# The weights' ring as one tile with 16-byte steps between its buffers, and x moved by 8 bytes for the second layer's experts

## The chip, the cores and the metric

The kernel runs on one core of one Trainium2 chip. The metric is the device time of one execution in microseconds. The core's engines run their own instruction streams and wait for one another by semaphores: PE (TensorE) multiplies matrices, DVE (VectorE), ACT (ScalarE) and POOL (GpSimd) work element by element, and SP (SyncE) issues the DMAs. PE's work appears twice in a profile: PEld is the load of a matrix of weights into the array, PE the matmul that streams the other operand through it. On-chip memory (SBUF) has 128 partitions; an address here is a byte offset inside a partition, the same in all of them. PSUM takes the matmuls' results.

## The reference

Two layers work on 256 frames of width 1024. Layer 0 mixes with multi-head latent attention, layer 1 with sparse attention whose keys a small indexer picks. Each is followed by a PEER mixer, which is where most of the time goes, and each result is added to 1.41 times the input and normalised:

```python
for i in range(DEPTH):
    m = _mla_mixer(x, ...) if i % N_MIXERS == 0 else _dsa_mixer(x, ...)
    x = _layernorm(DN_ALPHA * x + m, ln_gain[i, 0], ln_bias[i, 0])
    f = _peer(x, peer_w_q[i], peer_sub_keys[i], peer_w_down[i], peer_w_up[i])
    x = _layernorm(DN_ALPHA * x + f, ln_gain[i, 1], ln_bias[i, 1])

def _peer(x, w_q, sub_keys, w_down, w_up):       # 16384 experts, 8 heads
    q = (xt @ w_q).reshape(T, PEER_HEADS, 2, PEER_QDIM // 2)
    ...                                          # top 16 of two key tables, top 16 of their sums
    u = w_down[e_blk]
    a = jnp.einsum('td,ted->te', x_blk, u)
    hg = jax.nn.gelu(a, approximate=False) * g_blk
    return jnp.einsum('te,ted->td', hg, w_up[e_blk])
```

## The kernel before

**Dense experts.** The kernel doesn't gather the chosen experts. It multiplies x by all 16384 rows of `w_down` (128 blocks of 128 experts), applies the GELU, multiplies by a matrix that holds each frame's gates at its chosen experts and zero elsewhere, and multiplies the result by all of `w_up`. So each layer has 128 blocks of "down" (results named `d`) and 128 of "up" (results named `y`), and between the blocks of `d` the small fp16 matmuls `G` that place the gates.

**Split operands.** Each matmul of float32 data is made of three in the faster format fp32r: an operand is split into a high part, a copy rounded to fp32r, and a low part, the difference. `mm3` (line 258) issues high by high, high by low and low by high. x's parts are `xh` and `xl` (lines 194 and 195, 8 chunks of 256 columns each). In the down stage (`proj`, line 264) the weights' 128 columns are loaded into the array and x's 256 columns of one chunk are streamed: per block 8 chunks times 3, 24 matmuls of 256 columns. In the up stage (`rows`, line 289) x's place is taken by two blocks at a time of the gated GELU, split by `operand` (line 1109) into slots of `xh` and `xl`; they are loaded as weights, and 512 columns of the ring's block are streamed: 2 groups of frames, 3 passes, 2 halves, 12 matmuls of 512 columns per block.

**The ring.** All weights run through one `Stream` (line 52), in the order in which `ws.add` names them. A block of 128 x 1024 is loaded by a DMA on SP's queue into one of four `raw` buffers (`_load`, line 70), copied by ACT into a `hi` tile and subtracted by DVE (some blocks by POOL) into a `lo` tile (`_split`, line 88; `open` and `close`, lines 110 and 124, do the same in an order written out by hand for the blocks around a normalisation). `hi` and `lo` come from two pools of four buffers (lines 170 and 171), each 4096 bytes long; a new tile waits for the last reader of the tile that had its buffer. `get` (line 104) hands out a block and splits those up to three ahead. The first block is split by hand in `first` (line 1142) from tiles made at lines 1132 to 1134, and is cut off the stream's list at line 1138. `share` (line 97) gives every third block to POOL during the query projection of layer 1.

**What sets the order.** Each engine executes its stream in order, and the tile framework adds the waits that the reads and writes ask for. Around a normalisation (`finish`, line 381) the order is written by hand: the last four blocks of the projection run for the first 128 frames, then for the second; the new x is transposed by PE (`Turned`, line 355), split into `xh` and `xl`, and multiplied into the next stage's first four blocks. `out_proj` (line 660) calls `finish` for both attentions, with `start` 0 for layer 0 and 4 for layer 1. In both attentions the heads' outputs are kept in `xh` and `xl` as well (`oh, ol = xh, xl`, lines 689 and 822), since x itself is no longer needed there.

**Other operands.** In layer 0's query projection the matmuls `qn` and `qr` stream the normalised latent from four small tiles `V` and `U` (pool `ohp`, line 721) with weights from the ring. Apart from these two and the two attentions' inner matmuls, all large matmuls pair a buffer of the ring with `xh` or `xl`.

Of the kernel before, what the change touches and what calls it, by code (L numbers as in the profile page):

```python
# [11 lines left out]
F32R = mybir.dt.float32r  # L12
# [6 lines left out]
P = 128  # L19
T = 256  # L20
D = 1024
NC = D // P
# [22 lines left out]
WARM = 9  # L45
EARLY = 11264
GSCALE = 2.0 ** 14
DSA_POOL = 3
MAGIC = 12582912.0


class Stream:
# [13 lines left out]

    def add(self, src, w=D):
        self.blocks += [(src[i], w) for i in range(src.shape[0])]

    def _load(self, upto):  # L70
        while self.n_loaded <= min(upto, len(self.blocks) - 1):
            src, w = self.blocks[self.n_loaded]
            if self.n_loaded in self.early:
                t = self.early[self.n_loaded]
            else:
                t = self.raw.tile([P, D], F32, tag="raw", name=f"raw{self.n_loaded}")
                self.last = self.nc.sync.dma_start(t[:, :w], src).ins
            self.tiles.append(t)
            self.n_loaded += 1
# [8 lines left out]
    def _split(self, upto, pooled=False):  # L88
        nc = self.nc
        while self.n_split <= min(upto, len(self.blocks) - 1):  # L90
            w = self.blocks[self.n_split][1]
            self._load(self.n_split)
            raw = self.tiles[self.n_split][:, :w]
            hi = self.hi.tile([P, D], F32R, tag="hi", name=f"hi{self.n_split}")[:, :w]
            lo = self.lo.tile([P, D], F32R, tag="lo", name=f"lo{self.n_split}")[:, :w]
            self.act(lambda: nc.scalar.copy(hi, raw))  # L96
            if pooled or self.share and self.n_split % self.share == 0:
                nc.gpsimd.tensor_tensor(lo, raw, hi.bitcast(F32), op=ALU.subtract)
            else:
                self.dve(lambda: nc.vector.tensor_tensor(lo, raw, hi.bitcast(F32), op=ALU.subtract))  # L100
            self.ready.append((hi, lo))
            self.n_split += 1
# [7 lines left out]
    def open(self, queue):  # L110

        i = self.n_split
        assert i == self.n_taken
        self._load(i)
        raw = self.tiles[i]
        hi = self.hi.tile([P, D], F32R, tag="hi", name=f"hi{i}")
        lo = self.lo.tile([P, D], F32R, tag="lo", name=f"lo{i}")
        queue("act", lambda: self.nc.scalar.copy(hi, raw))
        self.ready.append((hi, lo))
        self.n_split += 1  # L120
        self.n_taken += 1
        return i
# [39 lines left out]
def tile_trunk(ctx: ExitStack, tc: tile.TileContext, ins, out: bass.AP):  # L162
    nc = tc.nc
    def pool(name, bufs, **kw):
        return ctx.enter_context(tc.tile_pool(name=name, bufs=bufs, **kw))

    lead = pool("lead", 1)
    wide = pool("wide", 1)
    raws = pool("raws", 4)
    his = pool("his", 4)  # L170
    los = pool("los", 4)
    big = pool("big", 1)
    const = pool("const", 1)
    dram = pool("dram", 1, space=bass.MemoryType.DRAM)
# [16 lines left out]
    ones = lead.tile([P, 16], F32, tag="ones", name="ones")[:, 0:1]  # L191
    mhalf = lead.tile([P, 16], F32, tag="mhalf", name="mhalf")[:, 0:1]
    keep = [dram.tile([P, D], F32, tag=f"x{t}", name=f"x{t}") for t in range(2)]
    xh = wide.tile([P, NC, T], F32R, tag="xh", name="xh")
    xl = wide.tile([P, NC, T], F32R, tag="xl", name="xl")
    place16 = const.tile([P, 2, T], F16, tag="place16", name="place16")
    gate16 = const.tile([P, T], F16, tag="gate16", name="gate16")
    rest = const.tile([P, T], F32, tag="rest", name="rest")
# [11 lines left out]
    nc.vector.memset(ones, 1.0)  # L210
    nc.vector.memset(mhalf, -0.5)

    ws = Stream(nc, raws, his, los)
    ws.add(ins["mla_h"][0:6])
    ws.add(ins["mla_qk"])
    ws.add(ins["mla_v"])
# [72 lines left out]
    def rows(o4, lhs, blk, start, stop, tiles=(0, 1)):  # L289

        h, l = blk
        lh, ll = lhs
        for t in tiles:
            tsl = slice(t * P, (t + 1) * P)
            todo = [(w, rr, i, n) for i, (w, rr) in enumerate(((lh, h), (lh, l), (ll, h))) for n in range(2)]
            if stop:
                todo.sort(key=lambda z: z[3])
            for w, rr, i, n in todo:
                ins = mm(o4[t][n], w[:, tsl], rr[:, n * 512 : (n + 1) * 512], start and i == 0, stop and i == 2)
        return ins  # L300

    def queue_of():

        last = {}

        def queue(engine, emit):
            with ExitStack() as order:
                if engine in last:
                    order.enter_context(tc.issue_after(last[engine]))
                ins = emit()  # L310
            last[engine] = ins.ins
            return ins

        return queue
# [66 lines left out]
    def finish(y4, lhs_of, n, g, b, x, spare, lead=None):  # L381

        blks = [ws.get(ahead=0) for _ in range(STAGGER)]
        queue = queue_of()
        last = None
        norms = []
        for t in range(2):  # L390
            with ExitStack() as order:
                if last is not None:
                    order.enter_context(tc.issue_after(last.ins))
                for i, blk in enumerate(blks):
                    k = n - STAGGER + i
                    last = rows(y4, lhs_of(k), blk, k == 0, k == n - 1, (t,))
            norms.append(Norm(queue, x[t], y4[t], g, b, spare[t], spare[2 + t], spare[4]))
        n0, n1 = norms
        n0.sums()
        n0.square()  # L400
        n0.centre()
        n0.scale()
        n0.result()
        if lead is None:
            n1.sums()
            n1.square()
            n1.centre()
            n1.scale()
            n1.result()
            for t in range(2):  # L410
                for h, q in enumerate((nc.sync, nc.scalar)):
                    s = slice(h * 512, (h + 1) * 512)
                    q.dma_start(out[t * P : (t + 1) * P, s], spare[t][:, s])
            return
        nc.sync.dma_start(keep[0], spare[0])
        queue("pe", lambda: last)
        x0, x1 = Turned(queue, 0, spare[0]), Turned(queue, 1, spare[1])
        blk = [ws.open(queue) for _ in range(3)]
        n1.sums()
        x0.high(0, 2)  # L420
        x0.high(1, 4)
        n1.square()
        x0.low(0)
        n1.centre()
        blk.append(ws.open(queue))
        n1.scale()
        x0.low(1)
        n1.result()
        nc.sync.dma_start(keep[1], spare[1])
        unit = lead(queue)  # L430

        def do(t, part, *ks):
            for k in ks:
                unit(t, part, k, ws.ready[blk[k]])

        do(0, "hh", 0, 1, 2)
        do(0, "lh", 0, 1, 2)
        do(0, "hh", 3)
        do(0, "lh", 3)
        x1.high(0, 2)  # L440
        x1.high(1, 4)
        do(1, "hh", 0, 1, 2, 3)
        ws.close(blk[0], queue)
        ws.close(blk[1], queue)
        x1.low(0)
        do(0, "hl", 0, 1)
        do(1, "lh", 0, 1)
        do(1, "hl", 0, 1)
        ws.close(blk[2], queue)
        x1.low(1)  # L450
        do(0, "hl", 2)
        do(1, "hl", 2)
        do(1, "lh", 2)
        ws.close(blk[3], queue)
        do(0, "hl", 3)
        do(1, "hl", 3)
        do(1, "lh", 3)
# [202 lines left out]
    def out_proj(oh, ol, g, b, x, spare, start):  # L660
        for h in range(start, HEADS - STAGGER):
            for t in range(2):
                project(oh, ol, h, t)
        y4 = begun.pop("y4")
        finish(y4, lambda h: (oh[:, h, :], ol[:, h, :]), HEADS, g, b, x, spare, lead_queries)

    def load_mask(ar):
# [139 lines left out]
    def dsa():  # L807
# [82 lines left out]
        for t in range(2):  # L890
            for n in range(2):
                nc.scalar.copy(v[:, t, n * 512 : (n + 1) * 512], v4[t][n])
        ws.share = DSA_POOL
        for h in range(0, HEADS, 2):
# [22 lines left out]
    def peer(li):  # L917
# [77 lines left out]
        def choose():  # L995
# [40 lines left out]
            gt, i1 = tail[:, 0:T], tail[:, T : 2 * T]  # L1036
            nc.vector.tensor_scalar(gt, pg[:, :T], GSCALE, None, op0=ALU.mult)
            nc.vector.tensor_copy(gate16, gt)
# [23 lines left out]
        def place(g4, done):  # L1062
# [8 lines left out]
            if done < P:  # L1071
                nc.scalar.mul(A[:, done:, tsl], pv[:, done:, :], 1.0 / GSCALE)
            if done:
                nc.vector.scalar_tensor_tensor(A[:, :done, tsl], pv[:, :done, :], 1.0 / GSCALE, A[:, :done, tsl],
                                               op0=ALU.mult, op1=ALU.mult)
# [54 lines left out]
    xt = Arena(arena, 30720).take(NC, T)  # L1130
    piece = [slice(c, c + 2) for c in range(0, NC, 2)]
    raw0 = raws.tile([P, D], F32, tag="raw", name="raw0")
    hi0 = his.tile([P, D], F32R, tag="hi", name="hi0")
    lo0 = los.tile([P, D], F32R, tag="lo", name="lo0")
    nc.sync.dma_start(raw0, ins["mla_h"][0])
    for c in range(0, NC, 4):
        last = nc.sync.dma_start(xt[:, c : c + 4, :], ins["xT"][c // 4])
    ws.blocks = ws.blocks[1:]
    with tc.issue_after(last.ins):
        ws._load(2)  # L1140

    def first(o):

# [129 lines left out]
```

## Time and profile before

| what | value |
|---|---|
| median of 2 runs | 1838.18 us (1838.15 to 1838.22) |
| span of the profiled execution | 1836.6 us |
| layer 0's `d` stage, first to last matmul | 147.3 to 548.6 us |
| layer 0's `y` stage | 548.4 to 896.6 us |
| layer 1's `y` stage begins | 1480.8 us |
| HBM traffic over the span | 182 GB/s |

The profile is of one execution with a span of 1836.6 us, from the first to the last recorded instruction. Its groups of instructions name the line that issues them, the result and the operands by the program's tile names, the shape, the count, the busy time of the group and the mean duration of one. A matmul's recorded duration is longer than the distance from one to the next, because they are pipelined; what a stage costs is that distance times the count. Line 253 is the helper that records all matmuls, so groups have to be told apart by the tiles' names. In these groups the matmul of `d` lists `xh` first and the ring's buffer second, whichever is streamed.

### The profile page before, as it was taken

Reading aid. Unit: us, or ns where it says so; the run is one execution under the profiler, and the core shown is the slowest. Engines: PE = TensorE matmul, PEld = TensorE weight load, DVE = VectorE, ACT = ScalarE, POOL = GpSimd, SP = SyncE. Lnnn points to the kernel's source line nnn. Section 1 sums busy time; section 2 is a strip of 40 time slices with the busy share of each in tenths; the row PEclk is TensorE's granted clock in tenths of the full one; section 3 lists DMA queues with packets and bytes.
Section 4 is the critical chain, followed back from the end, with each engine's and each line's share of the span. In section 5 each row is a group of like instructions: output and inputs, shape, how many; then the busy total and the mean of one; then the engine's idle time right before and its main releaser. Section 6 shows DMA issues by size and latency. Waiting matters only on the chain.

```text
span 1836.6 us, 32394 instructions
## 1 busy us (share of the span) xinstructions
PE 1824.8 (99%) x12495; PEld 1671.9 (91%) x12495; DVE 1317.8 (72%) x2348; ACT 1056.2 (58%) x1834; POOL 362.8 (20%) x265
## 2 busy tenths in 40 slices
PE   9999999999999999999999999999999999999998
PEld 8899999999998888888889899999999988888886
DVE  6689986788865555555688789957888765555555
ACT  6655456887764444444466555548877654444443
POOL 2002442445510000000022004504455300000000
PEclk9999999999999999999999999999999999999999
DMA  7554555444456555555646445554444475555553
GB/s 240 195 179 167 184 184 172 162 161 152 161 174 237 192 192 194 193 194 195 210 157 227 164 165 182 173 193 161 154 157 155 168 235 192 194 193 194 195 195 116
DMA packets 93468, 335.47 MB, mean 183 GB/s; under 512 B 10368, under 2 KB 11392, under 8 KB 93312
## 3 DMA queue, kind: packets, MB, share of 16 engines
q1 hardware_dynamic: 93024, 332.87, 52.9%
q8 instruction: 98, 1.61, 0.4%
q14 instruction: 58, 0.48, 0.1%
q10 hardware_dynamic: 288, 0.52, 0.1%
HBM read 329.16 MB, written 4.19 MB: 182 GB/s over the span
## 4 chain that ended last, share of the span: by engine, by line
PE 98%; DVE 1%; issue 1%; ACT 0%; DMA 0%; SPq 0%; DVEq 0%; POOLq 0%; POOL 0%; ACTq 0%
PE d L253 40%; PE y L253 40%; PE pq L253 4%; PE G L253 3%; PE q L253 3%; PE v L253 1%; PE qw L253 1%; PE s L253 1%; PE ps L253 1%; PE h L253 1%; PE qi L253 1%; PE o L253 1%; PE qn L253 0%; DMA arena<-in_xT 0%; PE kn L253 0%
## 5 line engine op out<-in xcount | busy, mean ns | idle before, releaser
L100 DVE TENSOR_TENSOR lo<-raw,hi 128x1024 fp32r<-128x1024 f32 (+1 forms) x579 | 763.9, 1321 | 345.0 <-ACT hi L96 344.1
L96 ACT CAST hi<-raw 128x1024 fp32r<-128x1024 f32 (+1 forms) x583 | 611.0, 1049 | 561.7 <-PE d L253 265.3
L253 PE MATMUL d<-xh,hi 128*128 128x256 f32 x2048 | 585.1, 286 | 0.0
L253 PE MATMUL d<-xh,lo 128*128 128x256 f32 x2048 | 579.2, 283 | 0.0
L253 PE MATMUL d<-xl,hi 128*128 128x256 f32 x2048 | 579.2, 283 | 0.0
L253 PEld LDWEIGHTS d<-xl,hi 128*128 128x128 f32 x2048 | 392.7, 192 | 0.0
L253 PEld LDWEIGHTS d<-xh,lo 128*128 128x128 f32 x2048 | 392.6, 192 | 0.0
L253 PEld LDWEIGHTS d<-xh,hi 128*128 128x128 f32 x2048 | 392.5, 192 | 0.0
L253 PE MATMUL y<-lo,xh 128*128 128x512 f32 x1088 | 337.7, 389 | 0.0
L253 PE MATMUL y<-hi,xh 128*128 128x512 f32 x1088 | 337.7, 390 | 0.0
L253 PE MATMUL y<-hi,xl 128*128 128x512 f32 x1088 | 337.3, 389 | 0.0
L1055 POOL TENSOR_TENSOR gate<-hot,gate 128x512 f16<-128x512 f16 x128 | 221.8, 1751 | 310.6 <-DVE hot L1053 310.6
L253 PEld LDWEIGHTS y<-lo,xh 128*128 128x128 f32 x1088 | 204.2, 188 | 42.7 <-DVE lo L100 0.3
L253 PEld LDWEIGHTS y<-hi,xl 128*128 128x128 f32 x1088 | 204.2, 188 | 42.4
L253 PEld LDWEIGHTS y<-hi,xh 128*128 128x128 f32 x1088 | 203.8, 188 | 41.8
L347 POOL TENSOR_TENSOR st<-st,mhalf 128x1 f32<-128x1 f32 x8 | 4.4, 551 | 827.2 <-DVE st L345 827.2
L1059 ACT ACTIVATE gate<-hot,rest 128x128 f16<-128x128 f16 x512 | 166.1, 413 | 0.9 <-DVE hot L1053 0.9
L1114 ACT CAST xh<-arena 128x512 fp32r<-128x512 f32 x128 | 79.8, 623 | 145.6 <-PE y L253 145.4
L1115 DVE TENSOR_TENSOR xl<-arena,xh 128x512 fp32r<-128x512 f32 x128 | 88.2, 692 | 73.5 <-ACT xh L1114 73.5
L1053 DVE TENSOR_TENSOR hot<-iota,place 128x1024 f16<-128x1024 f16 x128 | 84.9, 703 | 49.1 <-PE G L253 49.0
L1024 POOL TENSOR_TENSOR arena<-arena 128x800 f32<-128x800 f16 x32 | 78.8, 2482 | 38.8 <-DVE arena L1022 38.0
L253 PE MATMUL G<-gate,hot 128*128 128x128 f16 x1024 | 70.1, 221 | 0.0
(222 smaller groups left out, 1739.5 us busy)
## 6 DMA issues: line engine op xcount, KB each, us to landing
raw<-in_down SPq DMA_DIRECT2D x256, 512.0 KB, 3.2
raw<-in_up SPq DMA_DIRECT2D x256, 512.0 KB, 4.3
raw<-in_peer_q SPq DMA_DIRECT2D x24, 512.0 KB, 4.4
raw<-in_dsa_qk SPq DMA_DIRECT2D x16, 512.0 KB, 3.2
raw<-in_mla_w_o SPq DMA_DIRECT2D x8, 512.0 KB, 5.9
arena<-in_peer_q SPq DMA_DIRECT2D x8, 512.0 KB, 4.3
raw<-in_dsa_v SPq DMA_DIRECT2D x8, 512.0 KB, 4.3
raw<-in_dsa_w_o SPq DMA_DIRECT2D x8, 512.0 KB, 3.7
```

Source lines behind the costliest of these rows:

```text
L96: self.act(lambda: nc.scalar.copy(hi, raw))
L100: self.dve(lambda: nc.vector.tensor_tensor(lo, raw, hi.bitcast(F32), op=ALU.subtract))
L253: return pe(lambda: nc.tensor.matmul(o, l, r, start=start, stop=stop, skip_group_check=True))
L347: nc.gpsimd.tensor_tensor(st[:, 5:6], st[:, 4:5], mhalf, op=ALU.pow)
L1024: nc.gpsimd.tensor_tensor(o.rearrange("p k c -> p c k"), same, cell[t][:, h, :, None].to_broadcast([P, CELLS, TOPK]), op=ALU.mult)
L1053: nc.vector.tensor_tensor(hot, iota4[:, None].to_broadcast([P, 2, P, 4]), place16[:, :, None, four].to_broadcast([P, 2, P, 4]), op=ALU.is_ ...
L1055: nc.gpsimd.tensor_tensor(gate[:, 0], hot[:, 1].rearrange("p c j -> p j c"), gate16[:, four, None].to_broadcast([P, 4, P]), op=ALU.mult)
L1059: nc.scalar.mul(gate[:, 1, j, :], hot[:, 1, :, j], rest[:, t : t + 1])
L1114: nc.scalar.copy(hh, a)
L1115: nc.vector.tensor_tensor(al, a, hh.bitcast(F32), op=ALU.subtract)
```

## The change

The two pools of four tiles become two tiles, `hi` and `lo`, each with room for four buffers of 1024 columns and 64 columns more. Block i of the stream lies in buffer i modulo 4, at 4096 bytes times its number and 16 bytes times its number further. `xh` and `xl` become two halves of one tile, and a second pair of views of the same tile begins 2 columns, 8 bytes, later; `out_proj` of layer 1 turns to these views before its `finish`, so that the new x, layer 1's query projection and its experts use them. The heads' outputs that this projection reads stay in the first views. The first block is counted as block 0 of the stream now, so the indices of the others grow by one, and the test for POOL's blocks takes one off.

```diff
+RING = 4
+SKEW = 4
...
+    def parts(self, i):
+        skew = i % RING * SKEW
+        at = i % RING * D + skew
+        return [ring[:, at : at + self.blocks[i][1]] for ring in (self.hi, self.lo)]
...
-            hi = self.hi.tile([P, D], F32R, tag="hi", name=f"hi{self.n_split}")[:, :w]
-            lo = self.lo.tile([P, D], F32R, tag="lo", name=f"lo{self.n_split}")[:, :w]
+            hi, lo = self.parts(self.n_split)
             self.act(lambda: nc.scalar.copy(hi, raw))
-            if pooled or self.share and self.n_split % self.share == 0:
+            if pooled or self.share and (self.n_split - 1) % self.share == 0:
...
-    his = pool("his", 4)
-    los = pool("los", 4)
+    rings = pool("rings", 1)
...
-    xh = wide.tile([P, NC, T], F32R, tag="xh", name="xh")
-    xl = wide.tile([P, NC, T], F32R, tag="xl", name="xl")
+    xs = wide.tile([P, 2 * NC * T + 64], F32R, tag="xs", name="xs")
+    views = [xs[:, at : at + 2 * NC * T].rearrange("p (b c t) -> p b c t", c=NC, t=T) for at in (0, 2)]
+    xh, xl = views[0][:, 0], views[0][:, 1]
...
-    ws = Stream(nc, raws, his, los)
+    ring = [rings.tile([P, RING * D + 64], F32R, tag=k, name=k) for k in ("hi", "lo")]
+    ws = Stream(nc, raws, *ring)
...
         y4 = begun.pop("y4")
+        nonlocal xh, xl
+        if start:
+            xh, xl = views[1][:, 0], views[1][:, 1]
         finish(y4, lambda h: (oh[:, h, :], ol[:, h, :]), HEADS, g, b, x, spare, lead_queries)
...
-    hi0 = his.tile([P, D], F32R, tag="hi", name="hi0")
-    lo0 = los.tile([P, D], F32R, tag="lo", name="lo0")
...
-    ws.blocks = ws.blocks[1:]
+    hi0, lo0 = ws.parts(0)
+    ws.n_loaded = ws.n_split = ws.n_taken = 1
+    ws.tiles.append(raw0)
+    ws.ready.append((hi0, lo0))
     with tc.issue_after(last.ins):
-        ws._load(2)
+        ws._load(3)
```

`open` takes its `hi` and `lo` from `parts` in the same way as `_split`.

More of the change, by code (lines that the diff above doesn't have):

```diff
@@ L115, in open @@
         raw = self.tiles[i]
-        hi = self.hi.tile([P, D], F32R, tag="hi", name=f"hi{i}")
-        lo = self.lo.tile([P, D], F32R, tag="lo", name=f"lo{i}")
+        hi, lo = self.parts(i)
         queue("act", lambda: self.nc.scalar.copy(hi, raw))
```

## The prediction

> **What bounds the kernel now.** I read the page's busy rows first, then its slices, then the chain of work that ended last.
>
> ```profile
> span 1836.6 us, 32394 instructions
> PE 1824.8 (99%) x12495; PEld 1671.9 (91%) x12495; DVE 1317.8 (72%) x2348; ACT 1056.2 (58%) x1834; POOL 362.8 (20%) x265
> PEclk9999999999999999999999999999999999999999
> PE 98%; DVE 1%; issue 1%; ACT 0%; DMA 0%; SPq 0%; DVEq 0%; POOLq 0%; POOL 0%; ACTq 0%
> ```
>
> PE is busy in 99% of the span at full granted clock, and 98% of the chain is PE. So the time is a number of matmuls times the distance from one start to the next, and waits of the other engines cost nothing today. A busy PE is not PE at its peak, so the next view is the chain in order of time (start, us, what, count), where a group's time over its count is that distance.
>
> ```profile
> 23.94 2.16 PE krope L253 x18
> 26.10 4.10 PE qn L253 x36
> 35.20 4.25 PE qr L253 x36
> 151.56 146.63 PE d L253 x1222
> 548.60 348.19 PE y L253 x1536
> 1083.91 146.63 PE d L253 x1222
> ```
>
> An experts' first matmul d (256 columns) starts every 146.63/1222 = 0.1200 us in both layers; a second one, y (512 columns), every 348.19/1536 = 0.2267 us. The 256 columns between them cost 106.7 ns, so a column costs 0.417 ns, and both shapes carry the same rest: 120.0 - 106.7 = 13.3 ns and 226.7 - 213.4 = 13.3 ns. One weight load goes with each matmul of either shape. The rest is worth 13.3 ns on some 10,900 fp32r matmuls, 145 us, and the whole question is whether it depends on addresses.
>
> Two rows say that it can. krope, qn and qr are the same shape with the same kind of weights (slices of hi and lo). krope streams xh and xl: 2.16/18 = 120.0 ns. qn and qr stream the small tiles V and U instead: 4.10/36 = 113.9 and 4.25/36 = 118.1. In the program as compiled, xh, xl and all buffers of hi and lo start 1024 bytes past a multiple of 4096, so every load of weights and every stream of x begin on the same low address bits; V and U start 192 bytes past a multiple of 1024. The starts one by one:
>
> ```profile
> 31.42 0.28 PE L253 MATMUL qn<-V,lo 128*128 128x256 f32 x1
> ...
> 32.55 0.28 PE L253 MATMUL qn<-V,hi 128*128 128x256 f32 x1
> ```
>
> ```profile
> 35.98 0.28 PE L253 MATMUL qr<-V,lo 128*128 128x256 f32 x1
> ...
> 37.16 0.28 PE L253 MATMUL qr<-V,hi 128*128 128x256 f32 x1
> ```
>
> Ten steps each: 1.13 and 1.18 us, a steady 113 and 118 ns with the same addresses. So off the common address there is more than one rhythm, set by how the stage was entered. On the common address there is one, and it pulls:
>
> ```profile
> 317.62 0.36 PE L253 MATMUL d<-xh,hi 128*128 128x256 f32 x1
> 317.82 0.28 PE L253 MATMUL d<-xl,hi 128*128 128x256 f32 x1
> 317.93 0.28 PE L253 MATMUL d<-xh,lo 128*128 128x256 f32 x1
> 318.05 0.28 PE L253 MATMUL d<-xh,hi 128*128 128x256 f32 x1
> 318.17 0.28 PE L253 MATMUL d<-xl,hi 128*128 128x256 f32 x1
> ```
>
> After an interruption d starts at distances near 118 and is at 120 by the fourth. For y the transient is on the other side:
>
> ```profile
> 72.11 0.40 PE L253 MATMUL y<-lo,xh 128*128 128x512 f32 x1
> ...
> 73.51 0.39 PE L253 MATMUL y<-lo,xh 128*128 128x512 f32 x1
> ```
>
> Six steps in 1.40 us, 233 ns, against the settled 226.7. I read this as the load of the next weights and the running stream meeting in the memory, in a pattern that settles. It is a reading; the trace shows only distances.
>
> **The change part by part.** *Instructions.* Nothing is added or removed: the same copies, subtractions, loads of weights, matmuls and DMAs, in the same order. The block counter starts at 1 instead of 0, and the test for the pooled subtraction is shifted by one with it, so the same blocks go to POOL. Loading reaches the same block ahead. Cost: nothing, because no instruction differs.
>
> *Waits.* The rotating tiles become slices of one tile. A copy into a slice still has to wait for the matmuls that read that slice four blocks earlier, the same wait as for the tile. If instead the whole ring counted as one, each copy would wait for the block now running. These rows bound that: copy and subtraction would stand ahead of every block.
>
> ```profile
> L100 DVE TENSOR_TENSOR lo<-raw,hi 128x1024 fp32r<-128x1024 f32 (+1 forms) x579 | 763.9, 1321 | 345.0 <-ACT hi L96 344.1
> L96 ACT CAST hi<-raw 128x1024 fp32r<-128x1024 f32 (+1 forms) x583 | 611.0, 1049 | 561.7 <-PE d L253 265.3
> L1114 ACT CAST xh<-arena 128x512 fp32r<-128x512 f32 x128 | 79.8, 623 | 145.6 <-PE y L253 145.4
> ```
>
> That is 579 times (1049 + 1321) ns, 1372 us more, three quarters of the span. But the last row is already a slice of one tile, xh, written while PE reads other slices of it, and its 128 copies cost PE nothing. I take 0. The split halves of x share a tile after the change too; the view 8 bytes further is first written when the old view's last matmul has run, since PE's queue puts the transposes that feed it behind that matmul. Cost 0.
>
> *Weights' offset.* Buffers 1, 2 and 3 of the ring move by 16, 32 and 48 bytes, buffer 0 by nothing (the tiles' lengths move all of lo and hi by multiples of 256 besides). x stays in layer 0 and moves by 8 bytes from layer 1's query projection on, so that there all four buffers stand off it. Counted from the code: matmuls that read a buffer of the ring and xh or xl are, before the move of x, 4056 of 256 columns (h 120, krope 24, kn 48, pq 288, d 3072, qi 96, ki 24, q 384) and 1896 of 512 (y 1728, v 120, qw 48), and after it 3360 (pq, d) and 1584 (y, qw). Off the common address are three quarters of the first and all of the second: 0.75 x 4056 + 3360 = 6402 of 256 columns and 0.75 x 1896 + 1584 = 3006 of 512.
>
> No row shows offsets of 8 to 48 bytes. The nearest are qn and qr. For 256 columns the gain is then between 2 ns (120 - 118) and 7 ns (120 - 113) each, 13 to 45 us. I take the middle, 4.5 ns, since both rhythms were met at the same addresses: 6402 x 4.5 = 28.8 us. For 512 columns no row stands off the common address at all. The bounds are a loss of 6.3 ns (233 against 226.7) and the gain of 7; the 13.3 ns are the same in both shapes, so I take the same 4.5 ns: 3006 x 4.5 = 13.5 us. Ends: +19 to -21 us. Together 42 us. The 108 matmuls of qn and qr may move by up to 7 ns each, under 1 us.
>
> A floor for the rest is read from the fp16 matmuls of 128 columns:
>
> ```profile
> 316.88 0.93 PE G L253 x16
> ```
>
> 0.93/16 = 58 ns less 53.3 for the columns leaves 4.8 ns. So at most 13.3 - 4.8 = 8.5 ns can go: 9408 x 8.5 = 80 us. The Trainium skill, "TensorE: Matmul & The Clock Gate", section "Phases on the wall clock" under "Step-by-step", gives about 2.5 ns for this rest; by that page the most that could go would be an estimated 102 us, an end that I do not use.
>
> *What is late next.* The cover for the rest of the work, by windows (window, its length, then busy time of PE, PEld, DVE, ACT, POOL):
>
> ```profile
> 160.00:290.00 130.00, 130.00 (x1086) 130.00 (x1085) 111.45 (x332) 64.73 (x75) 49.93 (x48) 1.00 0.54 186
> 560.00:890.00 330.00, 330.00 (x1457) 273.26 (x1456) 188.96 (x180) 157.29 (x179) 0.00 (x0) 1.00 0.58 197
> ```
>
> DVE is the fullest, 111.45/130 = 86% beside d while the experts are chosen; with blocks 4% shorter it is at 89%, and at the floor of 8.5 ns at 92%. The DMA share of 0.54 to 0.58 rises as little. They still hide.
>
> **Sum.** The profiled execution is 1836.6 us of span, 1.6 under the runs' 1838.2. 1838.2 - 42.3 = 1795.9, so 1796 us.
>
> **The rivals.** *No change.* The rest of 13.3 ns is fixed per load, and V and U are faster for another reason than their address, or 16-byte steps don't matter where 192 do. For it: the same addresses gave 113 and 118. Against it: nothing else differs between krope and qn than the streamed tile. Time: 1838. The Trainium skill speaks for this rival: "SBUF — State Buffer", section "Who interferes with whom", gives PE two independent read ports, one for the stream and one for the weights, and says that PE never waits on anyone. By that rule the sum would be 0 and the time 1838; the trace agrees for DVE and ACT, which are busy beside d without moving its 120.0, and doesn't for the two streams of PE, if krope and qn differ by address.
>
> *Weak.* d goes to 118 and y stays: 6402 x 2 = 13 us, 1825.
>
> *Strong.* Every pair reaches 113 or better: 9408 x 7 = 66 us, 1772, with the floor at 1758.
>
> *Slower.* y loses its settled rhythm and stays at its transient's 233 ns, while d gains nothing: 3006 x 6.3 = 19 us, 1857. It decides as soon as y loses more than 2.1 times what d gains per matmul (6402/3006). For it: the transient of y above stands over 226.7 on the mean. Against it: they settle within some ten matmuls, and an offset is constant over the 12 of a block.
>
> *False waits.* The ring treated as one tile: 1838 + 1372 = 3210 us. Against it: xh above.
>
> **How the numbers follow.** Forecast 0.35, no change 0.2, weak 0.15, strong 0.17, slower 0.11, false waits 0.02. The forecast's own range is 1780 to 1812, d and y at 3 to 6 ns. The range 1765 to 1845 leaves out the strongest part of strong (0.06), most of slower (0.08) and the false waits. About 2%, 37 us, is what a measurement can tell from no change: faster means under 1801.4. That takes 0.28 of the forecast's 0.35 and nearly all of strong: 0.44. Slower by over 2% means above 1875, beyond the slower rival's 1857, unless d loses as well: 0.04 with the false waits. The remainder, 0.52, is within 2%.
>
> **What would show it.** The chain's rows for d and y, time over count: below 120.0 and 226.7 where a step holds, and different from block to block, as the buffers stand differently. In layer 0 every fourth block should stay at 120. Layer 1's d should be faster than layer 0's. If d and y keep 120.0 and 226.7, the address was not the reason; if PE shows idle time ended by ACT or DVE, the waits changed; if the windows beside d show DVE full, the cover is gone. The number of instructions should not change.

## The result, and the profile after

| | before | after |
|---|---|---|
| median | 1838.18 us | 1848.85 us (1848.69 to 1849.01) |
| ratio to before | | 1.0058 [1.004, 1.0077] |
| span of the profiled execution | 1836.6 us | 1847.2 us |

The change costs 10.7 us, 0.6%, where 42 us of gain were forecast. The page of the changed kernel: its head, the busy row, the granted clock, the chain by engine, and the costliest groups (busy us, mean ns of one, idle time before them and its releaser).

```profile
span 1847.2 us, 32393 instructions
PE 1835.2 (99%) x12495; PEld 1667.9 (90%) x12495; DVE 1317.4 (71%) x2348; ACT 1055.5 (57%) x1834; POOL 362.6 (20%) x265
PEclk9999999999999999999999999999999999999999
PE 98%; DVE 1%; issue 1%; ACT 0%; DMA 0%; SPq 0%; DVEq 0%; POOLq 0%; POOL 0%; ACTq 0%
L107 DVE TENSOR_TENSOR lo<-raw,hi 128x1024 fp32r<-128x1024 f32 (+1 forms) x579 | 763.7, 1321 | 350.5 <-ACT hi L103 349.4
L103 ACT CAST hi<-raw 128x1024 fp32r<-128x1024 f32 (+1 forms) x583 | 609.9, 1047 | 565.8 <-PE d L260 262.1
L260 PE MATMUL y<-hi,xs 128*128 128x512 f32 x2176 | 595.7, 393 | 0.0
```

Every engine executes the same number of instructions as before (PE 12495, DVE 2348, ACT 1834, POOL 265), at the same clock; the copies and subtractions take what they took (1047 and 1321 ns against 1049 and 1321), and the matmuls wait for nothing (0.0 in the last column). PE is busy 10.4 us longer with the same matmuls. So neither waits nor work explain the loss; the distances must. The chain of the changed kernel in order of time (start, us, what, count):

```profile
23.93 1.66 PE krope L260 x14
25.59 4.25 PE qn L260 x36
34.99 4.26 PE qr L260 x36
...
151.36 144.88 PE d L260 x1222
...
544.56 356.42 PE y L260 x1536
...
1088.11 146.79 PE d L260 x1222
...
1486.01 347.77 PE y L260 x1510
```

From the same view of the kernel before, the one row that the prediction didn't need:

```profile
1480.94 342.31 PE y L253 x1510
```

Time over count gives the distances. `d` goes from 120.0 to 118.6 ns in layer 0 (144.88/1222) and to 120.1 in layer 1. `y` goes from 226.7 to 232.0 in layer 0 and to 230.3 in layer 1. The stages add up to the loss, by the starts in these rows and in those of the prediction:

| stage | before | after | difference |
|---|---|---|---|
| layer 0, `d` and `G` (start of `d` to start of `y`) | 397.04 us | 393.20 us | -3.8 |
| layer 0, `y` | 348.19 | 356.42 | +8.2 |
| layer 1, `d` and `G` | 397.03 | 397.90 | +0.9 |
| layer 1, `y` | 342.31 | 347.77 | +5.5 |

Unrounded, the sum is +10.7 us, against +10.6 in the spans. The attentions between the layers keep their length: the end of layer 0's `y` and the start of layer 1's `d` both move by 4.2 us.

### The profile page after: what moved, and what is told of

The parts are those of the page before. It is cut to its first block, busy times and chain, and to the rows that moved or that the text cites. A ratio compares the mean times of both kernels' runs of the same rounds, so it can differ in the third digit from the quotient of the medians.

```text
span 1847.2 us, 32393 instructions
## 1 busy us (share of the span) xinstructions
PE 1835.2 (99%) x12495; PEld 1667.9 (90%) x12495; DVE 1317.4 (71%) x2348; ACT 1055.5 (57%) x1834; POOL 362.6 (20%) x265
## 4 chain that ended last, share of the span: by engine, by line
PE 98%; DVE 1%; issue 1%; ACT 0%; DMA 0%; SPq 0%; DVEq 0%; POOLq 0%; POOL 0%; ACTq 0%
PE y L260 41%; PE d L260 40%; PE pq L260 4%; PE G L260 3%; PE q L260 3%; PE v L260 1%; PE qw L260 1%; PE s L260 1%; PE ps L260 1%; PE h L260 1%; PE qi L260 1%; PE o L260 1%; PE qn L260 0%; PE kn L260 0%; DMA arena<-in_xT 0%
## 5 line engine op out<-in xcount | busy, mean ns | idle before, releaser
L107 DVE TENSOR_TENSOR lo<-raw,hi 128x1024 fp32r<-128x1024 f32 (+1 forms) x579 | 763.7, 1321 | 350.5 <-ACT hi L103 349.4
L103 ACT CAST hi<-raw 128x1024 fp32r<-128x1024 f32 (+1 forms) x583 | 609.9, 1047 | 565.8 <-PE d L260 262.1
L260 PE MATMUL d<-xs,hi 128*128 128x256 f32 x4096 | 742.5, 283 | 0.0
L260 PEld LDWEIGHTS d<-xs,hi 128*128 128x128 f32 x4096 | 632.1, 190 | 0.0
L260 PE MATMUL y<-hi,xs 128*128 128x512 f32 x2176 | 595.7, 393 | 0.0
L260 PE MATMUL d<-xs,lo 128*128 128x256 f32 x2048 | 576.5, 281 | 0.0
L260 PEld LDWEIGHTS y<-hi,xs 128*128 128x128 f32 x2176 | 408.4, 188 | 93.7
L260 PEld LDWEIGHTS d<-xs,lo 128*128 128x128 f32 x2048 | 388.0, 189 | 0.0
L260 PE MATMUL y<-lo,xs 128*128 128x512 f32 x1088 | 342.9, 394 | 0.0
L260 PEld LDWEIGHTS y<-lo,xs 128*128 128x128 f32 x1088 | 204.4, 188 | 47.0 <-DVE lo L107 0.3
L1124 ACT CAST xs<-arena 128x512 fp32r<-128x512 f32 x128 | 79.4, 620 | 151.6 <-PE y L260 148.8
L1125 DVE TENSOR_TENSOR xs<-arena,xs 128x512 fp32r<-128x512 f32 x128 | 88.3, 692 | 79.0 <-ACT xs L1124 79.0
```

The costliest lines, as they stand in the source:

```text
L260: return pe(lambda: nc.tensor.matmul(o, l, r, start=start, stop=stop, skip_group_check=True))
L1124: nc.scalar.copy(hh, a)
L1125: nc.vector.tensor_tensor(al, a, hh.bitcast(F32), op=ALU.subtract)
```

## The experiments

The theory after the result: the one tile and its waits cost nothing, and the addresses of the two operands set the distance, differently for 256 and for 512 columns. The rival: the one tile itself, or its shift by some hundred bytes, moves the distances, and the steps of 16 and 8 bytes do little. A second question was where the `d` gain stayed, above all in layer 1, which was forecast as the better layer. All edits are to the changed kernel.

In e4, e5, e7, e9 and e10 the offset changes between stages or within one. At such a change neighbouring buffers overlap by the step, so some columns of a few blocks can be overwritten before they are read; that changes part of what is computed, not the number of instructions. In e4, e5, e9 and e10 PE also takes the matmuls around such a change in another order.

**e1_flat: one tile, no offsets.** The ring's step is 0, and both views of x begin at 0.

```diff
-SKEW = 4
+SKEW = 0
...
-    views = [xs[:, at : at + 2 * NC * T].rearrange("p (b c t) -> p b c t", c=NC, t=T) for at in (0, 2)]
+    views = [xs[:, at : at + 2 * NC * T].rearrange("p (b c t) -> p b c t", c=NC, t=T) for at in (0, 0)]
```

> The ring stays one tile and x's halves one tile, but all buffers stand at offset 0 and x is not moved. Address theory (distances depend on where the loaded weights stand against the streamed operand): d back at 120.0 ns and y at 226.7 in both layers, 1838 us. Rival, the one tile (its waits, or the tiles' start 256 bytes later): the time stays at 1849, with y at 230 to 232 or with PE waiting.

Measured: 1838.32 us, ratio 1.0001 [0.9992, 1.0011]. Its chain in order of time:

```profile
150.94 146.63 PE d L260 x1222
...
547.98 348.19 PE y L260 x1536
...
1083.34 146.63 PE d L260 x1222
...
1480.36 342.31 PE y L260 x1510
```

All four rows have the times of before to 0.01 us. The rival falls: the one tile, its waits and the new place of everything by multiples of 256 bytes cost nothing. The offsets are the whole effect.

**e2_ring_only and e3_x_only: one offset each.** e2 keeps the ring's steps and leaves x at 0 (`(0, 0)` in the views). e3 has `SKEW = 0` and keeps x's 8 bytes in layer 1.

> The ring's buffers keep their 0, 16, 32 and 48 bytes, x is not moved for layer 1. Address theory: layer 1 becomes a copy of layer 0 of the changed kernel, d 118.6 ns instead of 120.1 and y 232.0 instead of 230.3: 4.6 us less and 2.6 us more, 1847 us. Rival, the 8 bytes of x are what costs: layer 1 has y at 226.7 and d at 118.6, 1839 us.

> All buffers at offset 0, x moved by 8 bytes in layer 1. Layer 0 as before the change (120.0 and 226.7). In layer 1 the offset is one constant, minus 8 bytes. If each offset has its own settled distance: layer 1 like the changed kernel's buffer 3 (minus 8 modulo 64 too), d near 118.0 and y near 233: 6 us less and 10 us more, 1841 us. If it is the change of offset from block to block that costs: y settles at 227 or less in layer 1 and the time is 1838 or below.

Measured: e2 1846.65 us, 1.0046 [1.003, 1.0063]; e3 1842.26 us, 1.0022 [1.0012, 1.0032]. The chain's rows for layer 1, of e2:

```profile
1087.61 144.84 PE d L260 x1222
...
1480.84 350.46 PE y L260 x1510
```

and of e3:

```profile
1083.85 146.64 PE d L260 x1222
...
1478.88 348.32 PE y L260 x1510
```

With the ring's steps alone, layer 1 looks like layer 0: `d` 118.5, `y` 232.1. With x's 8 bytes alone, the long stretch of `d` stays at 120.0 and `y` loses 4.0 ns (230.7). (After that stretch e3's `d` goes a little faster; its whole stage takes 1478.88 - 1083.85 = 395.03 us, 2.0 less than before.) So each offset costs `y`, the ring's steps help `d`, and with the 8 bytes on top that help is gone: together they gave 120.1. e3's time is close to the 1841 us expected, but by two misses that offset each other: neither 118 for all of `d` nor 233 for `y` came. The two losses don't add up (8.3 + 3.9 us over e1, against 10.5 for both): in layer 1 `y` loses 5.5 us with both offsets in place of 8.2 and 6.0, and `d`'s gains of 3.8 and 2.0 turn into a loss of 0.9.

**e4_sweep16 and e5_sweep4: each offset for a while.** All buffers of the expert stages stand at one offset, and it grows every 8 blocks by 16 bytes in layer 0 and by 8 in layer 1 (e4), or every 4 blocks by 4 bytes (e5). x stays at 0. PE waits at each change, which makes these runs longer (1994.04 and 2014.91 us), so only distances are read from them.

```diff
-        skew = i % RING * SKEW
+        skew = self.offset(i)
...
+    def offset(self, i):
+        for first in self.sweeps:
+            if first <= i < first + 128:
+                return (i - first) // 8 * (SKEW if self.sweeps.index(first) < 2 else SKEW // 2)
+        return 0
```

> One offset for all four buffers, changed every 8 blocks in the experts' stages: layer 0 by 16 bytes, 0 to 240; layer 1 by 8 bytes, 0 to 120. x is not moved. If every offset has its own settled distance, each stretch of 8 blocks shows one of its own, d between 113 and 122 ns and y between 224 and 236, repeating with some period in bytes. If only the change of offset costs, every stretch settles at 120.0 and 226.7 after its first block. If the offset modulo 64 bytes is all that counts, the four stretches 0, 64, 128 and 192 agree.

> One offset for all four buffers in the experts' stages, changed every 4 blocks by 4 bytes: 0 to 124 in layer 0, 128 to 252 in layer 1; x is not moved. Each change of offset makes PE wait about 1 us, because neighbouring buffers overlap at it, so only the distances count, not the time. Address theory: y is fastest at 0 (226.7) and stands at 229 to 235 everywhere else; d is slowest near 0 (120) and has its best between 113 and 116 near 64 and 88 bytes. If the 16-byte sweep's values were noise of the order of blocks, the offsets that both sweeps have would disagree by several ns.

Matmuls of `y` in e4's layer 0, from the timeline (start, us, operation, count; neighbours with the same operands share a row), at offsets 0, 16 and 32:

```profile
577.82 0.62 PE L269 MATMUL y<-lo,xs 128*128 128x512 f32 x2
...
590.05 0.62 PE L269 MATMUL y<-lo,xs 128*128 128x512 f32 x2
...
600.30 0.62 PE L269 MATMUL y<-hi,xs 128*128 128x512 f32 x2
...
620.69 0.39 PE L269 MATMUL y<-hi,xs 128*128 128x512 f32 x1
...
623.35 0.62 PE L269 MATMUL y<-hi,xs 128*128 128x512 f32 x2
...
643.86 0.40 PE L269 MATMUL y<-hi,xs 128*128 128x512 f32 x1
```

54 steps in 12.23 us are 226.5 ns at offset 0. 88 steps in 20.39 us are 231.7 ns at 16, and 88 in 20.51 are 233.1 at 32. In the same way, as the mean of the distances between the starts of all matmuls of one offset (interruptions of over 190 ns for `d` and 300 for `y` left out), in ns:

```
offset, bytes    0      16     32     48     64     128    192
d, layer 0     119.9  118.4  118.7  117.8  115.3  118.7  117.8
d, layer 1     120.0  118.4  118.3  118.0  115.1
y, layer 0     227.7  231.5  233.2  233.0  232.7  232.0  233.0
```

Over all sixteen offsets of layer 0, `y` is at 231.0 to 234.6 everywhere but at 0, and `d` is at its worst at 0: 115.3 to 119.8 elsewhere. In layer 1, `d` has its best at 64 and 88 bytes (115.1 and 113.9). The steps of 4 bytes in e5 show the same: `y` at 226.7 once settled at 0, and up to 237.7 elsewhere; `d` lowest at 64 and 76 (114.6 and 114.1). Each stretch keeps a level of its own, so it isn't the change of offset alone that costs; and 0, 64, 128 and 192 differ, so the offset modulo 64 isn't all that counts. The common address is `y`'s best in both sweeps and among the slowest for `d`. It is not `d`'s single worst: the finer steps have 121.0 at 24 bytes (e4, layer 1) and 120.8 at 220 (e5). The change gave both stages the same offsets.

The sweep gives the size of the loss too. The changed kernel's `y` in layer 0 has four offsets, whose constant values average (226.7 + 231.5 + 233.2 + 233.0)/4 = 231.1; it ran at 232.0. By the buffer that is streamed, its distances are 230.3, 231.4, 233.7 and 232.7: buffers 1 to 3 stand where the sweep has them, and buffer 0, at the good offset, loses 3.6 ns, now that blocks at other offsets run before and after it. 3.6/4 is the missing 0.9. Layer 1 doesn't follow the sweep so closely. By buffer, its `y` takes 230.4, 232.9, 231.1 and 226.8: buffer 3, at 48 bytes with x at 8, is as fast as the common address, where the sweep with x at 0 had 233.7 at the same difference of 40 bytes. So `y` can reach its best elsewhere too, and the difference of the two offsets alone doesn't fix its distance; whether x's own place or the blocks before and after it do, no run separates.

**e7_down_only: the ring's steps everywhere but in the up stages.** x at 0.

```diff
-        skew = i % RING * SKEW
+        skew = 0 if any(first <= i < first + 128 for first in self.ups) else i % RING * SKEW
```

> The ring's 0, 16, 32 and 48 bytes for all blocks but the up stages', which stand at 0; x is not moved. If the loss sits in the up stage alone: d at 118.6, y back at 226.7 in both layers, that is the ring-only kernel's 1846.7 less 5.3 ns x 3072 = 16 us, 1830. Rival, steps between buffers cost wherever they are used: no faster than 1838.

Measured: 1830.36 us, 0.9958 [0.9944, 0.9972]. The chain:

```profile
544.34 348.21 PE y L262 x1536
...
1079.27 144.84 PE d L262 x1222
...
1472.50 342.33 PE y L262 x1510
```

`y` is back at 226.7 in both layers and `d` keeps 118.5: e2 differs from this kernel by the steps in the up stages alone, and they cost it 16.3 us (1846.65 - 1830.36). Without them the ring's steps are a small gain. Against the changed kernel e7 is 18.5 us faster: 8.2 + 5.5 of `y`, and 4.7 of layer 1's `d` stage (397.90 to 1472.50 - 1079.27 = 393.23), which is the 8 bytes of x.

**e6_x168 and e8_x192: move x instead of the ring.** `SKEW = 0`; x stands at 168 or 192 bytes in all projections of both layers, the heads' outputs and the up stages' operands at 0. The difference of the addresses in e6 is that of e9 below modulo 256.

```diff
-    views = [xs[:, at : at + 2 * NC * T].rearrange("p (b c t) -> p b c t", c=NC, t=T) for at in (0, 2)]
-    xh, xl = views[0][:, 0], views[0][:, 1]
+    views = [xs[:, at : at + 2 * NC * T].rearrange("p (b c t) -> p b c t", c=NC, t=T) for at in (0, 48, 48)]
+    xh, xl = views[1][:, 0], views[1][:, 1]
+    kept = views[0][:, 0], views[0][:, 1]
...
-        oh, ol = xh, xl
+        oh, ol = kept
...
-                hh, al = xh[:, slot, :], xl[:, slot, :]
+                hh, al = kept[0][:, slot, :], kept[1][:, slot, :]
```

In e6 the views are at `(0, 42, 42)`.

> All buffers at 0; x stands 168 bytes into its tile in all projections of both layers, so that the weights stand 88 bytes past it modulo 256; the heads' outputs and the up stage's operands stay at 0. If the offset between the two operands counts, whichever is moved: d, pq and q at 113.9 ns as in the sweep at 88 bytes, 6.1 ns x 7300 = 45 us less, y stays at 226.7, 1794 us. Rival, the address of the loaded weights alone counts: d stays at 120.0 and the time at 1838.

> As the kernel with x at 168 bytes, with x at 192: the weights stand 64 bytes past x modulo 256, as V and U have it. If this is the same pairing as in qn and qr, d, pq and q take one of their two rhythms, 113.4 or 117.8 ns: 7300 matmuls at 6.6 or 2.2 ns less are 48 or 16 us, less 1.4 us lost in v and qw, 1791 or 1823. Rival, moving x never helps (as at 168): d at 120.0 and 1839.5 us.

Measured: e6 1839.64 us, 1.0008 [0.9998, 1.0018], a miss. e8 1818.50 us, 0.9895 [0.9878, 0.9911], the fastest version here and ahead of both kernels. Of e6's chain the row of `d`:

```profile
150.91 146.64 PE d L261 x1222
```

and of e8's chain:

```profile
149.19 86.77 PE d L261 x765
...
238.13 1.14 DVE lo L107
...
253.05 38.14 PE d L261 x334
...
537.42 348.21 PE y L261 x1536
...
1069.87 143.93 PE d L261 x1222
```

168 bytes leave `d` at 120.0, as its rival said, by which the weights' address alone counts. 192 bytes exclude that rival: the weights stand as in e6, and `d` takes 113.4 (86.77/765) in a part of layer 0 and 117.8 in layer 1, the two rhythms of `qn` and `qr`, at the same addresses. And at 113.4 something new shows: the chain leaves PE for DVE. Windows of e8 (window, its length, busy time of PE, PEld, DVE, ACT, POOL, granted clock, DMA share, GB/s):

```profile
150.00:235.00 85.00, 85.00 (x752) 85.00 (x752) 84.01 (x349) 47.28 (x55) 35.27 (x43) 1.00 0.55 178
```

The same window of the kernel before:

```profile
150.00:235.00 85.00, 85.00 (x711) 85.00 (x710) 82.18 (x344) 44.24 (x52) 32.18 (x41) 1.00 0.53 181
```

DVE was at 97% in these 85 us already, while experts are chosen, and its `lo` blocks still came in time. At 99%, with 752 matmuls in place of 711, some no longer do: the chain goes through `lo` at 238 us. The 86% that the prediction read was a mean with the emptier time after 235 us.

**e9_down88 and e10_down64: the sweep's best offsets, held.** All buffers at 88 (e9) or 64 bytes (e10) in the two down stages, at 0 elsewhere; x at 0.

```diff
-        skew = i % RING * SKEW
+        skew = 22 if any(first <= i < first + 128 for first in self.downs) else 0
```

> The buffers stand 88 bytes into their slots for the two down stages and at 0 for all else; x is not moved. If the sweeps' 113.9 and 115.8 ns at this offset hold over a whole stage: 6144 matmuls at 4.2 to 6.1 ns less, 26 to 37 us, 1801 to 1812. If a long stage falls into a rhythm of 120 ns, as with x at 168 bytes, which is the same difference between the two operands: 1838.

> As the kernel at 88 bytes, with 64. The sweeps gave 115.3, 115.1 and 114.6 ns there, a mixture of steps of 113 and 118: 6144 x 4.7 to 5.4 ns = 29 to 33 us less, 1805 to 1809; at a pure 113 it would be 1797, at a pure 118 1826, and 1838 if a long stage falls back to 120.

Measured: e9 1818.64 us, 0.9894 [0.9878, 0.9911]; e10 1819.17 us, 0.9901 [0.9884, 0.9917]. The two and e8 can't be told apart. `d` holds the sweep's level: without interruptions the mean is 114.8 and 115.0 ns in e9's layers. Five ns on 6144 matmuls would be 31 us, and 19.4 came, short of the 1801 to 1812 and 1805 to 1809 us expected. Where the rest went, by the windows beside the choosing of the experts and after it, first of e1:

```profile
147.00:300.00 153.00, 153.00 (x1278) 153.00 (x1277) 127.17 (x391) 75.91 (x88) 49.81 (x48) 1.00 0.55 183
300.00:538.00 238.00, 238.00 (x2239) 236.54 (x2238) 192.33 (x239) 182.25 (x461) 110.89 (x64) 1.00 0.48 159
```

then of e9:

```profile
147.00:300.00 153.00, 151.38 (x1296) 149.51 (x1295) 132.30 (x392) 76.93 (x90) 46.72 (x48) 1.00 0.55 183
300.00:538.00 238.00, 238.00 (x2312) 236.69 (x2311) 197.38 (x242) 187.12 (x468) 110.84 (x64) 1.00 0.50 167
```

After 300 us PE fits 73 more matmuls into the window, 3.3%; before it 18, 1.4%, and PE is idle 1.6 us. There DVE is late. Rows of waits of e9 (us in total, times, longest), of PE and of the loads of weights:

```profile
PE d L262 <- DVE lo L107: 2.9, 5, 1.2
PE pq L262 <- ACT hi L103: 2.0, 2, 1.0
PE pq L262 <- DVE lo L107: 0.8, 1, 0.8
PEld d L262 <- DVE lo L107: 6.3, 18, 1.3
```

In the two layers PE waits 2.9 us for `lo` and the loads of weights 6.3 us, 18 times. In layer 0's `d` there are 57 distances over 190 ns, against 37 in e1, and the sum of the distances between neighbouring `d` matmuls falls by 11.5 us instead of the 15.5 of the mean. With 11.8 us in layer 1 that is 23.3, while the span falls by 18.2 (1836.0 to 1817.8). Much of the 5 us between is lost at the starts of the `d` stages, where the offset changes. There PE takes the last blocks of `pq` among the first of `d`, and waits 2.8 us by the two `pq` rows, which e1 doesn't have: counted from the first matmul of `pq`, the 150th of `d` comes 0.8 and 2.1 us later than in e1, though its distances are shorter.

**e11_x48_x248 and e12_after_x16: why layer 1's 8 bytes help nothing.** e11 is e6 with x at 48 bytes in layer 0 and 248 in layer 1, `(0, 12, 62)`. Either the difference of the two addresses counts, or x's own place, 8 bytes past a multiple of 16, is bad whatever the ring's. e12 is the changed kernel with 16 bytes for x instead of 8, `(0, 4)`.

> As the kernels with x at 168 and 192 bytes, but x at 48 bytes in layer 0 and at 248 in layer 1; the weights then stand 208 and 8 bytes past x modulo 256, where the sweeps with x at 0 gave 116.7 and 116.4 ns for d. If the difference of the two operands is what counts: about 116.6 in both layers, 7300 x 3.4 = 25 us less, 1815 with the 1.4 us of v and qw. If a streamed operand that begins 8 bytes past a multiple of 16 brings 120 ns back (x at 8 and at 168 bytes did): 116.7 in layer 0, 120.0 in layer 1, about 1827.

> The changed kernel with x moved by 16 bytes instead of 8 in layer 1. If it is the 8 bytes off a multiple of 16 that took the gain from layer 1's d: d there as in layer 0, 118.6 instead of 120.1, 4.6 us less; y stays between 230 and 232, so 1844 to 1847. If any move of x does it: d at 120 again and 1849 with y as it was.

Measured: e11 1833.67 us, 0.9975 [0.9966, 0.9985]; e12 1844.45 us, 1.0033 [1.002, 1.0046]. The chain of e11:

```profile
151.22 144.60 PE d L261 x1222
...
1078.66 146.65 PE d L261 x1222
```

and of e12:

```profile
1087.30 144.21 PE d L260 x1222
...
1478.92 350.22 PE y L260 x1510
```

At 48 bytes `d` has 118.3, at 248 it has 120.0. That is the second reading, with 118.3 where the sweep let 116.7 be expected, and so 1833.67 us in place of 1827. At 16, with the ring's steps, it has 118.0, where 8 gave 120.1. All four stages with x 8 bytes past a multiple of 16 (8 with and without the ring's steps, 168, 248) stand at 120.0 to 120.1 in the long stretch, and the three with x at such a multiple other than 0 (16 with the ring's steps, 48, 192) are below. This is shown for these seven, not for others, and for the long stretch alone: in the rest of its stage e3's `d` takes 118.6 on the mean, at the same addresses. The difference alone doesn't decide: 88 bytes by the ring gave 114.8, the same 88 modulo 256 by x gave 120.0.

## Why the prediction was wrong

**What bounds the kernel: right.** PE is still 99% busy, and the time moved with distances times counts: the four stages give 10.7 us for the 10.6 of the span.

**Instructions and waits at nothing: right.** The counts are the same, and e1 ran in 1838.32 us with the one tile. ("In the same order" isn't quite so: between 47 and 59 us, in layer 0's attention, PE's order differs at 28 places, in e1 as well.) The false waits (3210 us) are excluded by it.

**That addresses set the rest of 13.3 ns: right.** The rival "no change" is excluded: offsets alone moved the whole from 1818.5 (e8) to 1848.85 us. The Trainium skill, "SBUF — State Buffer", section "Who interferes with whom", gives PE's stream and its weights independent read ports, and by it, as the prediction read it, the sum would be 0. The runs disagree with 0: e1 and the changed kernel differ in addresses alone, and by 10.5 us.

**The step that failed: "the 13.3 ns are the same in both shapes, so I take the same 4.5 ns".** An equal rest at one common address says nothing of how the two shapes answer when they leave it. `y` is at its best there, 226.7, and no stretch of any run was faster. Off it, 5.3 ns are lost in layer 0 and 3.6 in layer 1, where 4.5 were to be gained: this term came out at +13.7 us for the two `y` stages in place of -13.5 for all of 512 columns. The bound on that side, +6.3 ns from the six steps of 233, was nearly the answer: in layer 0 buffers 1 to 3 run at 231.4 to 233.7. The transient of `y` was the nearest row for its own shape, and the prediction preferred a row of the other shape. What it held against the slower rival, that the matmuls settle within some ten, holds at offset 0 only; with the offsets they settle elsewhere.

**The size of the 256-column term: too large.** The middle of 113 and 118 was taken, from tiles at 192 bytes. The weak rival's 2 ns were close: 120.0 to 118.6 in layer 0. In the forecast's own terms all 256-column matmuls should have gained 28.8 us, 24.2 of them in `d` (3072 x 0.75 x 4.5 ns and 3072 x 4.5 ns); the two `d` stages gained 3.8 and lost 0.9.

**Every fourth block at 120 in layer 0: right.** By buffer, `d` there takes 119.6, 118.4, 118.4 and 117.8 ns.

**Layer 1's `d` faster than layer 0's: wrong.** It stayed at 120.1 (by buffer 118.0, 119.7, 120.8 and 121.9). Standing off the common address isn't enough: with x 8 bytes past a multiple of 16 the long stretch stood at 120 in e3, e6 and e11 too, with the ring at 0.

**"They still hide": right for this change, wrong at the distances that the prediction allowed.** At 118.6 ns nothing came late. At 113 to 115 DVE did (e8, e9). The prediction's 86%, and its 92% at the floor, were means over 130 us of uneven load: the first 75 of them were 98% full (73.6 us). The strong rival's 1772 us came in no run: `y` was nowhere below 226.7, and late DVE work took a part of `d`'s gain in e8 and e9. How much freeing DVE would give back, no run tried.

**Which rival came.** The slower one, by its mechanism: `y` off its rhythm. Its price was 1857 us with nothing gained by `d`; `d`'s small gain in layer 0, and a smaller loss of `y` in layer 1, make it 1848.85, beyond the range's end of 1845.

**What stays open.** Which part of the chip makes these distances. The runs show that they depend on where both operands begin, that the common address is `y`'s best and among `d`'s slowest, and that two rhythms can hold at one pair of addresses. What picks the rhythm, and why layer 1's buffer 3 has `y` at 226.8, stays open as well.

## What to carry to other kernels

Price a change of addresses by the stage and by the shape: the place that is best for one pair of operands can be among the worst for another, so offsets are set for each stage alone (the ring's steps without the up stages, e7, are 16 us better than with them, e2). A shape's own transient is a nearer row than another shape's steady state. When the bounding engine gets 5% faster, look at the next engine in the fullest hundred microseconds, not over the stage.

## What was not expected of the hardware

- With the same instructions, 256 columns in fp32r start every 113.4 to 121.9 ns and 512 every 226.7 to 237.7, on the mean of a stretch or a buffer, with nothing but the operands' byte offsets changed.
- One pair of addresses holds more than one rhythm: 113.4 and 117.8 ns in the two layers of e8.
- A good offset loses its rhythm among others: buffer 0's `y` in layer 0 at 230.3 instead of 226.7. In layer 1 another pair, the ring at 48 and x at 8, has 226.8.
- 16 bytes for x instead of 8 are worth 4.4 us of 1848.85 (e12).
